# A mixture-of-experts layer: where rows are split for the gather, which buffers are withheld, how many banks the gather turns through, where the loop of further passes stands, and the order of the last step

## The chip, the cores and the metric

The kernel runs on one core of a Trainium2 chip. The metric is the time of one execution on the device, in microseconds (us); the time before is the median of three runs, 1381.6 us (1379.36 to 1382.24).

## The reference

One decoder layer on 256 rows of 2048 numbers, float32 throughout. Causal attention with 16 heads, then `x <- LayerNorm(alpha * x + y)`, then a mixture of 32 experts, then a second such norm. Cut to what matters here, the mixture is:

```python
g_logits = xt @ w_grp + b_grp                  # 4 groups, the best one is taken
e_logits = einsum('td,dge->tge', xt, w_rt)     # 8 experts in it, the best two are taken
comb     = onehot_g[:, :, None] * e_gate[:, None, :]
for g in range(4):
    h = silu(einsum('td,edf->tef', xt, w_gate[g])) * einsum('td,edf->tef', xt, w_up[g])
    y = y + einsum('tef,efd->td', h * comb[:, g, :, None], w_down[g])
```

Each expert has three matrices of 2048 x 512 numbers (4.2 MB each), so the 32 experts are 403 MB that have to be read once; the attention's weights are another 67 MB.

## The kernel before

**Attention.** Weights come through three buffers of 16 KB per partition and are split in two float32r parts on ScalarE and VectorE before TensorE multiplies. None of this part is touched.

**Experts.** Each expert gets room for 64 rows. A step p handles experts 2p and 2p+1, 16 steps in all. In a step, `gather` picks the 64 + 64 rows of the two experts out of the normed rows by products with a one-hot matrix, which puts them transposed into `xg`; VectorE and ScalarE take the sums out of PSUM in turn and apply gain and offset. `gate_up` multiplies `xg` with the gate and up weights, two products at a time beside each other in the array; `hidden` forms silu(gate) * up * weight; `transpose_hidden` turns the result; `second_products` multiplies with the down weights; `add_rows` (called `rest(n)`, one quarter of the columns at a time) scatters the products back to the 256 rows and adds them to `acc`. The `rest` of step p runs between the gate and up products of step p+1, by way of `between`. The gather of step p+1 stands between `gate_up` and `second_products` of step p.

**Rows.** The normed rows are `xn` in float32 (one buffer). Step 0 gathers from `xn`. In step 0 `split_rows_in_three` turns `xn` into three bfloat16 parts (`xb`: two in `hm`, the third in half of the buffer that also holds `xg`), and all later steps gather from the three parts, three products where `xn` took one.

**Buffers.** SBUF is cut in twelve buffers ("slots") of 16 KB per partition. An expert's matrix comes as two loads of 2 MB, each filling one slot. `pieces` lists the loads in order: gate and up of a step, then its down weights; `advance` issues the next ones, on the SyncE queue, whenever `used` hands back slots that TensorE has finished with. Ten slots start the list (`S_FIRST`). Slots 0, 1 and 3 are not handed back once their first load is used (`S_SUM` for `acc`, `S_HM` for `hm`, `S_YS` for `ys_all`), slot 7 holds `xg` and the third part, and slot 4 (`xn`) joins the list in step 0 once the rows are split. So eight slots go round from then on.

**Loop.** An expert with more than 64 rows is served by a loop of further passes (`further_passes`), with a number of rounds read at run time; it stands behind step 10 (`LOOP_AFTER`) and keeps three slots back from loading (`LOOP_SLOTS`, L743 and L768). No weight loads of the loop appear in the trace: it ran no round. The residual alpha * x is added to `acc` in steps 11 and 12, two quarters in each (`RES_AT`, L789 to L792).

**Last step.** The gate and up products of step 15 stand ahead of the second products of step 14, and so do the loads (L418 to L421, L827 to L830). `last_norm` prepares gain and offset of the second norm, ahead of the second products of step 14. The last down weights come in five blocks of columns (`l`), so that the norm can begin early; behind the last products stand the quarters of `rest` of step 14 (L895 to L904).

**Order.** From the last block of the attention's output product on, ScalarE, VectorE and GpSimd run in the order of the code, and from the first gather on TensorE and SyncE too. Each engine is a queue: what stands ahead in the code and waits holds up what follows it on that engine.

Of the kernel before, what the change touches and what calls it, by code (L numbers as in the profile page):

```python
# [29 lines left out]
LOOP_AFTER = 10  # L30
RES_AT = (11, 12)
LOOP_SLOTS = 3
# [6 lines left out]
S_X, S_XT, S_OH, S_OL, S_QK, S_WS, S_TV, S_RING = 0, (1, 2), 3, 4, 5, (6, 7), 8, (9, 10, 11)  # L39


S_XN, S_XG, S_HM, S_SUM, S_YS = S_OL, S_WS[1], S_XT[0], S_X, S_OH
S_FIRST = S_XT + (S_QK,) + S_RING + (S_TV, S_WS[0], S_YS, S_SUM)
# [12 lines left out]
def hybrid_kernel(ctx: ExitStack, tc: tile.TileContext, x, w_qkv, w_o, ln1_g, ln1_b, w_grp, b_grp,  # L56
# [10 lines left out]
    def halves(i, name, dt=F32):  # L67
        t = slot(i, [P, 2, D], name, dt)
        return [t[:, 0], t[:, 1]]
# [82 lines left out]
    ws = Rot([h for i in S_WS for h in halves(i, f"ws{i}", F32R)])  # L152
# [289 lines left out]

    def used(*keys, keep=0):
        free.extend(place[k] for k in keys if place[k] not in (S_HM, S_SUM, S_YS))
        advance(keep)

# [81 lines left out]
    gub, mb, yb = Rot([0, 1]), Rot([2, 3]), (4, 5, 6, 7)  # L528

    def gather(c2, xg, o2, name, xn=None):  # L530
# [19 lines left out]
    def split_rows_in_three():  # L550

        for n in range(2):
            for tt in range(NT):
                t = xn[:, tt, n]
                for i in range(2):
                    nc.scalar.copy(xb[i][:, tt, n], t)
                    nc.vector.tensor_sub(t if i == 0 else xb[2][:, tt, n], t, xb[i][:, tt, n])
# [28 lines left out]
    def gate_up(gu, side, xg, j, wg, wu):  # L586

        for c in range(4 * (j % 2), 4 * (j % 2) + 4):
            st, sp = j == 0 and c == 0, j == 3 and c == 7
            for w, to in ((wg, sides[1 - side]), (wu, sides[side])):  # L590
                nc.tensor.matmul(gu[to], xg(8 * (j // 2) + c), w[:, c, :], start=st, stop=sp, skip_group_check=True)  # L591
# [46 lines left out]
    def residual(n, t):  # L638
# [3 lines left out]
        for tt in range(NT):  # L642
            g_ = rows_of(0, n, yb[2 * tt], f"g1_{n}_{tt}")
# [6 lines left out]
        b_ = rows_of(1, n, yb[0], f"b1_{n}")  # L650
# [24 lines left out]
    def further_passes(slots):  # L675

        ring = Rot(slots[1:])
        n_pass = nc.values_load(passes_i[0:1, 0:1], min_val=0, max_val=8,
                                skip_runtime_bounds_check_because="512 choices in passes of 64 leave at most 7")
        with tc.For_i(0, n_pass, 1, iteration_sync="staggered"):  # L680
# [24 lines left out]
            spare = slot(slots[0], [P, 2, D], "spare")  # L705
            xgx = spare[:, 0, 0:1024].rearrange("p (n e s) -> p n e s", n=NCH, e=1)
# [6 lines left out]
            for j in range(4):  # L713
                if j % 2 == 0:
                    wg, wu = [load([v[one, j // 2].rearrange("o p c f -> p (o c) f")], f"x{i}_{j}", ring())
                              for i, v in enumerate((wg_v, wu_v))]
                gate_up(gu, 0, lambda c: xgx[:, c, 0], j, wg, wu)
# [3 lines left out]
            for k in range(4):  # L721
                if k % 2 == 0:
                    wd = load([wd_v[one, k // 2].rearrange("o p i d -> p (o i) d")], f"xd_{k}", ring())
# [9 lines left out]
    xg_lo = halves(S_XG, "xg_lo")  # L733
    xg = xg_lo[0].rearrange("p (n e s) -> p n e s", n=NCH, e=2)
# [4 lines left out]
    gatef, gate3, xb, o2, scratch, ys_all, acc, rest = (None,) * 8  # L739

    def first_products(p):

        keep = LOOP_SLOTS if p == LOOP_AFTER else 0  # L743
# [233 lines left out]
```

## Time and profile before

| | |
|---|---|
| median of 3 runs | 1381.6 us |
| the profiled execution, its own time | 1382.03 us |
| its span, first to last instruction | 1380.3 us |
| TensorE busy with matmuls | 1307.1 us, 95% of the span |
| VectorE, ScalarE busy | 36%, 25% |
| bytes moved | 475.47 MB, mean 344 GB/s |
| granted TensorE clock, mean | 0.984 |

The profiled execution's own time is 1.7 us more than its span and 0.4 us above the median. TensorE's matmuls are pipelined and their ends are modelled, so 95% busy doesn't say that TensorE is the limit: in the same profile the DMA engines move 425 to 428 GB/s in nearly all slices from the fifteenth on. The page's chain of waits, followed back from the end, names who was last at each point, and the windows say how much was moved in a stretch.

### The profile page before, as it was taken

To read this page: it belongs to the slowest core of one execution; us is meant where nothing else is said; L and a number is where in the kernel's file an instruction comes from. 1 tells how busy PE (TensorE), PEld (TensorE's weight loads), DVE (VectorE), ACT (ScalarE), POOL (GpSimd) and SP (SyncE) were. 2 spreads that over 40 slices of the span, in tenths; PEclk is the share of its full clock that TensorE was granted. 3 is DMA by queue.
4 is the path that set the end of the run, shared out by engine and by line. 5 is a ranking of instruction groups with operands and counts; after the bars stand their busy time and mean duration, and the time that the engine had idled before them with its cause. 6 is when DMAs were issued, how large, how long until landed. Compare 5 with 4: busy or idle time off the path is not lost. (4 is left out here: it accounts for less than half of the span.)

```text
span 1380.3 us, 17486 instructions
## 1 busy us (share of the span) xinstructions
PE 1307.1 (95%) x7433; PEld 738.5 (53%) x7433; DVE 495.8 (36%) x869; ACT 347.6 (25%) x598; POOL 18.1 (1%) x59
## 2 busy tenths in 40 slices
PE   8999999999999999999999999999998799999996
PEld 7888888888896434434434343443433243443432
DVE  5564555545444422122221212222123336222136
ACT  4454534445325301101101010110101010111232
POOL 1000030000000000000000000000000000000000
PEclk9999999999999999999999999999999899999998
DMA  9745545477357999999999999999999999999993
GB/s 320 238 152 185 174 143 185 161 255 270 123 219 278 379 428 426 425 428 425 428 426 426 428 426 426 427 426 427 427 427 425 374 427 426 420 426 424 426 404 118
DMA packets 91829, 475.47 MB, mean 344 GB/s; under 512 B 9252, under 2 KB 48228, under 8 KB 67684
## 3 DMA queue, kind: packets, MB, share of 16 engines
q1 hardware_dynamic: 91748, 474.32, 85.6%
q8 instruction: 60, 0.98, 0.3%
q14 instruction: 21, 0.17, 0.0%
HBM read 472.20 MB, written 2.10 MB: 344 GB/s over the span
## 5 line engine op out<-in xcount | busy, mean ns | idle before, releaser
L591 PE MATMUL gu<-wu,xg_lo 128*64 128x512 f32 x1024 | 465.6, 605 | 15.1 <-DMA wu<-in_moe_w_up_dram 15.1
L591 PE MATMUL gu<-wg,xg_lo 128*64 128x512 f32 x1024 | 465.5, 604 | 8.2 <-PEq L680 8.2
L591 PEld LDWEIGHTS gu<-wg,xg_lo 128*64 128x64 f32 x1024 | 135.6, 138 | 198.7 <-issue 193.5
L764 PE MATMUL y<-wd,ht 128*64 128x512 f32 x960 | 211.4, 594 | 2.7 <-DMA wd<-in_moe_w_down_dram 2.0
L591 PEld LDWEIGHTS gu<-wu,xg_lo 128*64 128x64 f32 x1024 | 135.5, 138 | 100.6 <-issue 68.2
L210 PE MATMUL pj<-xt,ws 128*128 128x512 f32 x512 | 185.0, 403 | 0.0
L163 DVE TENSOR_TENSOR ws<-ring,ws 128x1024 fp32r<-128x1024 f32 x96 | 117.5, 1224 | 128.0 <-ACT ws L162 127.9
L211 PE MATMUL pj<-xt,ws 128*128 128x256 f32 x512 | 147.3, 288 | 0.0
L764 PEld LDWEIGHTS y<-wd,ht 128*64 128x64 f32 x960 | 68.0, 137 | 135.1 <-issue 129.1
L162 ACT CAST ws<-ring 128x1024 fp32r<-128x1024 f32 x96 | 101.1, 1053 | 138.6 <-PE pj L210 59.1
L627 DVE TENSOR_TENSOR acc<-acc,cb 128x512 f32<-128x512 f32 x112 | 71.9, 683 | 171.6 <-PE cb L617 171.6
L210 PEld LDWEIGHTS pj<-xt,ws 128*128 128x128 f32 x512 | 97.7, 191 | 21.8
L610 ACT CAST ys_all<-y 128x512 fp32r<-128x512 f32 x60 | 35.1, 585 | 290.7 <-PE y L764 158.5
L539 PE MATMUL pg<-o_dt.bfloat,hm 128*128 128x128 bf16 x960 | 88.3, 219 | 18.2 <-DVE xg_lo L546 15.5
L611 DVE TENSOR_TENSOR ys_all<-y,ys_all 128x512 fp32r<-128x512 f32 x60 | 41.2, 687 | 174.5 <-ACT ys_all L610 174.5
L211 PEld LDWEIGHTS pj<-xt,ws 128*128 128x128 f32 x512 | 98.5, 192 | 0.3
L539 PEld LDWEIGHTS <-hm 128*128 128x128 bf16 x960 | 75.3, 98 | 37.8 <-issue 37.1
L599 DVE SCALAR_TENSOR_TENSOR hs<-hs,gs,gu 64x512 f32<-64x512 f32 x32 | 23.9, 747 | 191.9 <-ACT hs L598 191.5
L539 PE MATMUL pg<-o_dt.bfloat,xg_lo 128*128 128x128 bf16 x480 | 84.3, 219 | 0.0
L598 ACT ACTIVATE hs<-gu 64x512 f32<-64x512 f32 x32 | 18.9, 591 | 219.5 <-PE gu L591 219.0
L548 ACT ACTIVATE xg_lo<-pg,gbp 128x128 f32<-128x128 f32 x128 | 51.6, 453 | 78.1 <-PE pg L539 78.1
L546 DVE TENSOR_SCALAR xg_lo<-pg,gbp 128x128 f32<-128x128 f32 x128 | 46.6, 406 | 66.2 <-PE pg L539 66.0
(229 smaller groups left out, 1285.3 us busy)
## 6 DMA issues: line engine op xcount, KB each, us to landing
wg<-in_moe_w_gate_dram SPq DMA_DIRECT2D x64, 2048.0 KB, 19.1
wu<-in_moe_w_up_dram SPq DMA_DIRECT2D x64, 2048.0 KB, 23.6
wd<-in_moe_w_down_dram SPq DMA_DIRECT2D x60, 2048.0 KB, 23.3
ring<-in_attn_w_qkv_dram SPq DMA_DIRECT2D x46, 1024.0 KB, 5.3
ring<-in_attn_w_o_dram SPq DMA_DIRECT2D x16, 1024.0 KB, 5.3
wl<-in_moe_w_down_dram SPq DMA_DIRECT2D x6, 1024.0 KB, 15.0
xs<-in_x_dram SPq DMA_DIRECT2D x8, 256.0 KB, 6.8
wl<-in_moe_w_down_dram SPq DMA_DIRECT2D x4, 512.0 KB, 11.5
```

Source lines behind the costliest of these rows:

```text
L162: nc.scalar.copy(t[:, 0, c], src[:, c])
L163: nc.vector.tensor_sub(t[:, 1, c], src[:, c], t[:, 0, c].bitcast(F32))
L210: nc.tensor.matmul(ps[i], w[:, 0], x2, start=c == 0, stop=False, skip_group_check=True)
L211: nc.tensor.matmul(ps[i][:, 0], w[:, 1], x2[:, 0], start=False, stop=c == NCH - 1, skip_group_check=True)
L539: nc.tensor.matmul(pg[:, cc], part[:, tt, n, c], o2[:, tt].rearrange("p e s -> p (e s)"), start=tt == i == 0, stop=tt == 1 and i == len(pa ...
L546: nc.vector.tensor_scalar(to, pg[:, cc], g_, b_, op0=ALU.mult, op1=ALU.add)
L548: nc.scalar.activation(to, pg[:, cc], AF.Identity, scale=g_, bias=b_)
L591: nc.tensor.matmul(gu[to], xg(8 * (j // 2) + c), w[:, c, :], start=st, stop=sp, skip_group_check=True)
L610: nc.scalar.copy(ys[0:rows, 0, 0:width], y[0:rows, 0:width])
L611: nc.vector.tensor_sub(ys[0:rows, 1, 0:width], y[0:rows, 0:width], ys[0:rows, 0, 0:width].bitcast(F32))
L627: nc.vector.tensor_add(t, t, cb)
L764: nc.tensor.matmul(y[n][sides[side]], ht[:, k, sides[side]], held["d", 2 * p + side, k // 2][:, k % 2, n * 512:(n + 1) * 512], start=k == ...
```

## The change

- `xn` stays in its slot until step 4. The gathers for steps 1 to 3 multiply `xn` in float32 (`o2f`, one-hots in float32) as that for step 0 does; the three bfloat16 parts are made in step 3 (`SPLIT_AT`), a quarter at each of the places i = 3 to 6, into the two slots whose weights step 3 has just used (`take`). Gathers from step 4 on use the parts.
- Slot 7 is cut in two halves of its own, one for `xg` and one for `ys_all`. In step 0 only one slot is not handed back, that of down weight (1, 1), for `acc`.
- `gather` turns through four PSUM banks (6, 7, 2, 3; in step 0: 4, 5, 2, 3) rather than two (2, 3). Step 0's last four gathers stand behind i = 1 instead of two each behind i = 0 and i = 1.
- The loop stands behind step 9 and keeps back one slot instead of three; the residual is added in steps 10 to 13, one quarter each, in banks 4, 5 and 6.
- Step 14 and step 15 run in plain order: second products of 14, `last_norm`, gate and up of 15; the loads follow the same order.

```diff
-LOOP_AFTER = 10
-RES_AT = (11, 12)
-LOOP_SLOTS = 3
+SPLIT_AT = 3
+LOOP_AFTER = 9
+RES_AT = (10, 11, 12, 13)
...
-        if pr == NP - 1:
-            pr -= 1
-        elif pr == NP - 2:
-            continue
-        for k in range(2):
-            pieces += [(("d", e, k), [wd_v[e, k]]) for e in (2 * pr, 2 * pr + 1)]
+        if pr < NP - 1:
+            for k in range(2):
+                pieces += [(("d", e, k), [wd_v[e, k]]) for e in (2 * pr, 2 * pr + 1)]
...
     def used(*keys, keep=0):
-        free.extend(place[k] for k in keys if place[k] not in (S_HM, S_SUM, S_YS))
+        free.extend(place[k] for k in keys if k not in taken)
         advance(keep)
...
+    wide, first_banks = Rot([6, 7, 2, 3]), Rot([4, 5, 2, 3])
-        pg = bank(mb(), [P, 2, m], f"pg{name}_{c2}")
-        parts = [xn] if xn is not None else xb
+        pg = bank((banks or mb)(), [P, 2, m], f"pg{name}_{c2}")
+        parts = [xn] if o2.dtype == F32 else xb
...
-        if p == 0 and i < 2:
-            for c2 in (2 * i + 4, 2 * i + 5):
-                gather(c2, xg, o2f, 0, xn)
         if p == 0 and i == 1:
+            for c2 in range(4, 8):
+                gather(c2, xg, o2f, 0, first_banks)
             gatef, gate3 = gates()
...
-            split_rows_in_three()
-        if p == 0 and i == 4:
+        if p == SPLIT_AT and i == 0:
+            take(("g", 2 * p, 0), ("u", 2 * p, 0))
+        if p == SPLIT_AT and i == 1:
+            hm, lo = [slot(place[k, 2 * p, 0], [P, 2, NT, 2, 8, P], f"part_{k}", BF16) for k in "gu"]
+            xb, spare = [hm[:, 0], hm[:, 1], lo[:, 0]], lo[:, 1].rearrange("p t n c a -> p (t n c a)").bitcast(F32)
+        if p == SPLIT_AT and 3 <= i < 7:
+            split_rows_in_three(*divmod(i - 3, 2))
+        if p == SPLIT_AT + 1 and i == 1:
             free.append(S_XN)
             advance()
...
-        if p in RES_AT and i in (4, 6):
-            if i == 4:
-                scratch = sm.tile([P, 64, 8], F32, name=f"xn_{p}", tag="ptv")
-            residual(2 * RES_AT.index(p) + (i - 4) // 2, scratch)
+        if p in RES_AT and i == 5:
+            residual(RES_AT.index(p), sm.tile([P, 64, 8], F32, name=f"xn_{p}", tag="ptv"))
...
-        if p == NP - 2:
-            rest = None
-            hs, last_ot, _ = first_products(p + 1)
-            five, offs = last_norm()
+        if p == 0:
+            place_acc, = take(("d", 1, 1))
         y = second_products(p, ht)
...
-            further_passes(list(free)[:LOOP_SLOTS])
+            further_passes(free[0])
             advance()
-    p, ot = NP - 1, last_ot
+    five, offs = last_norm()
+    hs, ot, *_ = first_products(NP - 1)
+    p, rest = NP - 1, None
...
-    for n in range(2):
-        rest(n)
     for n in range(len(blocks)):
         last_down(n)
...
-            for i in range(2, 4):
-                rest(i)
```

**The order of the loads, first step.** On the SyncE queue, from the first down weight on (the names are wg, wu, wd for gate, up and down, then expert and half; PE, DVE and DMAHW name whom the load waits for), before:

```order
L433 DMA wd_0_0_3261<-in_moe_w_down_dram 128x4096
L433 DMA wd_1_0_3272<-in_moe_w_down_dram 128x4096 [waits DVE_49,Activation_49]
L433 DMA wd_0_1_3395<-in_moe_w_down_dram 128x4096 [waits PE_49]
L433 DMA wd_1_1_3478<-in_moe_w_down_dram 128x4096 [waits DMAHW1_49,PE_49]
L433 DMA wg_2_0_3480<-in_moe_w_gate_dram 128x4096 [waits DMAHW2_49,PE_49]
L433 DMA wu_2_0_3505<-in_moe_w_up_dram 128x4096 [waits DMAHW3_49,DVE_49]
L433 DMA wg_2_1_3515<-in_moe_w_gate_dram 128x4096 [waits DMAHW4_49,PE_49]
```

The same loads in the changed kernel:

```order
L430 DMA wd_0_0_3262<-in_moe_w_down_dram 128x4096
L430 DMA wd_1_0_3273<-in_moe_w_down_dram 128x4096 [waits DVE_49,Activation_49]
L430 DMA wd_0_1_3382<-in_moe_w_down_dram 128x4096 [waits PE_49]
L430 DMA wd_1_1_3384<-in_moe_w_down_dram 128x4096 [waits DMAHW1_49,PE_49]
L430 DMA wg_2_0_3464<-in_moe_w_gate_dram 128x4096 [waits DMAHW2_49,PE_49]
L430 DMA wu_2_0_3466<-in_moe_w_up_dram 128x4096 [waits DMAHW3_49,PE_49]
L430 DMA wg_2_1_3502<-in_moe_w_gate_dram 128x4096 [waits DMAHW4_49,PE_49]
```

The loads keep their order. The up weight wu_2_0 waited for VectorE (the split rows, in the slot of `xn`) and now waits for TensorE; the last number of a name counts the program's instructions, and by it wd_1_1 moves to directly behind wd_0_1, and wu_2_0 to directly behind wg_2_0: each pair is now released at one place.

**The order of the loads, the loop.** On the SyncE queue, the last loads ahead of the loop and the wait in front of it, before:

```order
L433 DMA wd_21_1_6637<-in_moe_w_down_dram 128x4096 [waits DMAHW1_49,PE_49]
L433 DMA wg_22_0_6639<-in_moe_w_gate_dram 128x4096 [waits DMAHW2_49,PE_49]
L433 DMA wu_22_0_6730<-in_moe_w_up_dram 128x4096 [waits DMAHW3_49,PE_49]
L433 DMA wg_22_1_6732<-in_moe_w_gate_dram 128x4096 [waits DMAHW4_49,PE_49]
L433 DMA wu_22_1_6750<-in_moe_w_up_dram 128x4096 [waits DMAHW5_49,PE_49]
L433 DMA wg_23_0_6752<-in_moe_w_gate_dram 128x4096 [waits DMAHW6_49,PE_49]
L678 TENSOR_LOAD passes_i_3324 [waits DVE_49]
L680 COMPARE_AND_BRANCH [waits barrier_Pool_Activation_PE_DVE_SP_release,DMAHW0_49,DMAHW1_49,DMAHW7_49]
```

The same place in the changed kernel:

```order
L430 DMA wd_19_1_6129<-in_moe_w_down_dram 128x4096 [waits DMAHW5_49,PE_49]
L430 DMA wg_20_0_6131<-in_moe_w_gate_dram 128x4096 [waits DMAHW6_49,PE_49]
L430 DMA wu_20_0_6149<-in_moe_w_up_dram 128x4096 [waits DMAHW7_49,PE_49]
L430 DMA wg_20_1_6151<-in_moe_w_gate_dram 128x4096 [waits DMAHW0_49,PE_49]
L430 DMA wu_20_1_6242<-in_moe_w_up_dram 128x4096 [waits DMAHW1_49,PE_49]
L430 DMA wg_21_0_6244<-in_moe_w_gate_dram 128x4096 [waits DMAHW2_49,PE_49]
L430 DMA wu_21_0_6262<-in_moe_w_up_dram 128x4096 [waits DMAHW3_49,PE_49]
L430 DMA wg_21_1_6264<-in_moe_w_gate_dram 128x4096 [waits DMAHW4_49,PE_49]
L682 TENSOR_LOAD passes_i_3325 [waits DVE_49]
L684 COMPARE_AND_BRANCH [waits barrier_Pool_Activation_PE_DVE_SP_release,DMAHW0_49,DMAHW1_49,DMAHW5_49,DMAHW6_49,DMAHW7_49]
```

Five loads stood between the step's last down weight and the loop, seven stand there now. The branch in front of the loop waited for three DMA semaphores, none of which stands beside one of those five loads (they name DMAHW2 to DMAHW6); now it waits for five, and four of them (DMAHW6, 7, 0, 1) stand beside the first four of the seven loads.

**The end, on TensorE.** From the transposed hidden of step 15 to the first block of the last down weights (hp15 is the transposed hidden of step 15, cb14 a scatter of step 14's products, y15_0 the first block), before:

```order
L604 MATMUL hp15_8632<-ident_85,hs15_8474 128x128 x3
L616 MATMUL cb14_0_0_8641<-ys_all_3708,ot14_8272 128x512 [waits DVE_49]
L617 MATMUL cb14_0_0_8641<-ys_all_3708,ot14_8272 128x512
L616 MATMUL cb14_0_1_8645<-ys_all_3708,ot14_8272 128x512 [waits DVE_49]
L617 MATMUL cb14_0_1_8645<-ys_all_3708,ot14_8272 128x512
L616 MATMUL cb14_1_0_8651<-ys_all_3708,ot14_8272 128x512 [waits DVE_49,Activation_49]
L617 MATMUL cb14_1_0_8651<-ys_all_3708,ot14_8272 128x512
L616 MATMUL cb14_1_1_8655<-ys_all_3708,ot14_8272 128x512 [waits DVE_49]
L617 MATMUL cb14_1_1_8655<-ys_all_3708,ot14_8272 128x512
L867 MATMUL y15_0_8661<-wl_0_8545,ht15_8637 64x512 [waits DMAHW5_49,Activation_49]
L867 MATMUL y15_0_8661<-wl_0_8545,ht15_8637 64x512 [waits DMAHW6_49]
L867 MATMUL y15_0_8661<-wl_0_8545,ht15_8637 64x512 x6
```

The same place in the changed kernel:

```order
L595 MATMUL gu15_1_8359<-wg_31_1_8338,xg_3332 64x512
L595 MATMUL gu15_1_8359<-wu_31_1_8387,xg_3332 64x512
L609 MATMUL hp15_8492<-ident_85,hs15_8360 128x128 [waits DVE_49]
L609 MATMUL hp15_8492<-ident_85,hs15_8360 128x128 x3
L870 MATMUL y15_0_8501<-wl_0_8389,ht15_8497 64x512 [waits DMAHW7_49,Activation_49]
L870 MATMUL y15_0_8501<-wl_0_8389,ht15_8497 64x512 [waits DMAHW0_49]
L870 MATMUL y15_0_8501<-wl_0_8389,ht15_8497 64x512 x6
L870 MATMUL y15_1_8517<-wl_1_8426,ht15_8497 64x512 [waits DMAHW1_49]
L870 MATMUL y15_1_8517<-wl_1_8426,ht15_8497 64x512 [waits DMAHW2_49]
L870 MATMUL y15_1_8517<-wl_1_8426,ht15_8497 64x512 x6
```

The eight scatters shown, and eight more of step 14 that stood between the blocks y15_0 and y15_1, are gone from here (they stand between the gate and up products of step 15 now), and the transposed hidden follows directly on the gate and up products that it depends on.

## Rows read from the trace of the kernel before

**Rows 1.** The page: GB/s moved in 40 equal slices of the span.
```profile
GB/s 320 238 152 185 174 143 185 161 255 270 123 219 278 379 428 426 425 428 425 428 426 426 428 426 426 427 426 427 427 427 425 374 427 426 420 426 424 426 404 118
```

**Rows 2.** Windows: length, busy per engine, granted clock, DMA share, GB/s.
```profile
434.00:448.00 14.00, 14.00 (x74) 5.72 (x76) 5.92 (x27) 4.79 (x9) 0.00 (x0) 1.00 0.47 171
...
458.00:463.00 5.00, 4.11 (x38) 2.04 (x35) 3.81 (x9) 4.32 (x7) 0.00 (x0) 1.00 0.43 105
...
700.00:1050.00 350.00, 329.62 (x1818) 140.30 (x1815) 75.13 (x152) 44.25 (x92) 0.00 (x0) 0.99 1.01 427
...
1070.00:1080.00 10.00, 4.78 (x12) 1.64 (x14) 0.52 (x2) 0.00 (x0) 0.71 (x7) 0.54 0.65 239
```

**Rows 3.** Timeline of the SyncE queue, first step: start, length, load, count.
```profile
417.83 29.06 SPq L433 DMA_DIRECT2D wd<-in_moe_w_down_dram  x4
446.99 0.62 SPq L433 DMA_DIRECT2D wg<-in_moe_w_gate_dram  x1
460.08 0.33 SPq L433 DMA_DIRECT2D wu<-in_moe_w_up_dram  x1
```

**Rows 4.** Timeline of TensorE, step 0: two gather pieces from float32 rows.
```profile
431.90 2.05 PE L539 MATMUL pg<-o_dt.float,xn 128*128 128x128 f32 x16
```

**Rows 5.** Chain of waits (start, length, what): one gather from three parts.
```profile
1285.10 0.34 PE r L634 x4
...
1289.14 0.74 DVE xg_lo L546 x2
...
1292.39 1.50 PE pg L539 x24
1293.89 13.88 PE gu L591 x64
```

**Rows 6.** Tile hm: the splitting of the rows (ns min/median/max, first and last start).
```profile
L556 ACT CAST hm<-xn x8: 1028/1043/1045, 441.9 to 457.8; 128x1024 bf16<-128x1024 f32 x8
...
L557 DVE TENSOR_TENSOR xg_lo<-xn,hm x4: 1224/1224/1224, 448.4 to 458.8; 128x1024 bf16<-128x1024 f32 x4
```

**Rows 7.** Timeline of the SyncE queue at the loop.
```profile
1050.41 0.33 SPq L433 DMA_DIRECT2D wg<-in_moe_w_gate_dram  x1
1075.24 0.34 SPq L433 DMA_DIRECT2D wu<-in_moe_w_up_dram  x1
```

**Rows 8.** Waits from 1040 to 1090 us: waiting, waited for, us, times, longest.
```profile
PE gu L591 <- PEq L680: 8.2, 1, 8.2
```

**Rows 9.** Chain of waits: starts of steps 11 to 14 on TensorE.
```profile
1075.22 16.80 PE gu L591 x64
...
1133.60 3.43 PE gu L591 x16
...
1195.51 3.43 PE gu L591 x16
...
1249.98 3.43 PE gu L591 x16
```

**Rows 10.** Chain of waits at the end.
```profile
1308.03 7.04 PE gu L591 x32
1315.07 15.65 DMA wd<-in_moe_w_down_dram
...
1330.76 7.08 PE y L764 x30
1337.84 0.59 PE hp L604 x4
...
1341.01 3.61 PE y L867 x16
...
1347.93 3.58 PE y L867 x16
```

**Rows 11.** Timeline of ScalarE: `last_norm`, its first operation.
```profile
1322.60 2.00 ACT L808 ACTIVATE raw<-wv,rows 5x2048 f32<-5x2048 f32 x1
```

**Rows 12.** Timeline of VectorE: `last_norm`, its last long operation.
```profile
1331.32 2.34 DVE L813 SCALAR_TENSOR_TENSOR five<-raw,rows,five 5x2048 fp32r<-5x2048 f32 x1
```

More of the change, by code (lines that the diff above doesn't have):

```diff
@@ L67, in halves @@
     def halves(i, name, dt=F32):
+        if i == S_LOW:
+            return [slot(f"{i}{k}", [P, D], f"{name}{k}", dt) for k in range(2)]
         t = slot(i, [P, 2, D], name, dt)
@@ L149, in transpose_x @@
         nc.vector.tensor_sub(xt[i][:, k:k + 2, 1], pt, hi.bitcast(F32))
-    ws = Rot([h for i in S_WS for h in halves(i, f"ws{i}", F32R)])
+    ws = Rot([h for i in (S_WS, S_LOW) for h in halves(i, f"ws{i}", F32R)])
     def split_w(wt, half, name, pieces=1, factor=None):
@@ L441, in advance, with take @@
             held[key] = load(srcs, "w" + "_".join(map(str, key)), place[key])
+    taken = set()
     def used(*keys, keep=0):
-        free.extend(place[k] for k in keys if place[k] not in (S_HM, S_SUM, S_YS))
+        free.extend(place[k] for k in keys if k not in taken)
         advance(keep)
+    def take(*keys):
+        taken.update(keys)
+        return [place[k] for k in keys]
     advance(keep=1)
@@ L548, in gather, with split_rows_in_three @@
                 nc.scalar.activation(to, pg[:, cc], AF.Identity, scale=g_, bias=b_)
-    def split_rows_in_three():
-        for n in range(2):
[L553 to L557, printed above, removed]
+    def split_rows_in_three(n, tt):
+        t = xn[:, tt, n]
+        nc.scalar.copy(xb[0][:, tt, n], t)
+        nc.vector.tensor_sub(t, t, xb[0][:, tt, n])
+        nc.scalar.copy(xb[1][:, tt, n], t)
+        nc.vector.tensor_sub(xb[2][:, tt, n], t, xb[1][:, tt, n])
     def in_three(t, part, rest_):
@@ L584, in slots_of, with gate_up @@
         return ot, gs
-    def gate_up(gu, side, xg, j, wg, wu):
-        for c in range(4 * (j % 2), 4 * (j % 2) + 4):
-            st, sp = j == 0 and c == 0, j == 3 and c == 7
+    def gate_up(gu, side, xg, j, wg, wu, at):
+        for c in range(4):
             for w, to in ((wg, sides[1 - side]), (wu, sides[side])):
-                nc.tensor.matmul(gu[to], xg(8 * (j // 2) + c), w[:, c, :], start=st, stop=sp, skip_group_check=True)
+                nc.tensor.matmul(gu[to], xg(4 * j + c), w[:, at + c, :], start=j == c == 0, stop=j == c == 3,
+                                 skip_group_check=True)
     def hidden(gu, side, gs, hs):
@@ L673, in gates, with further_passes @@
         return gate, gate3
-    def further_passes(slots):
-        ring = Rot(slots[1:])
+    def further_passes(last):
         n_pass = nc.values_load(passes_i[0:1, 0:1], min_val=0, max_val=8,
@@ L713, in further_passes @@
             for j in range(4):
[L714 to L717, printed above, removed]
+                c = slice(4 * (j % 2), 4 * (j % 2) + 4)
+                w = load([v[one, j // 2][:, :, c].rearrange("o p c f -> p (o c) f") for v in (wg_v, wu_v)], f"x{j}", last)
+                gate_up(gu, 0, lambda c: xgx[:, c, 0], j, w[:, 0], w[:, 1], 0)
             hidden(gu, 0, gs, hs)
@@ L722, in further_passes @@
                 if k % 2 == 0:
-                    wd = load([wd_v[one, k // 2].rearrange("o p i d -> p (o i) d")], f"xd_{k}", ring())
+                    wd = load([wd_v[one, k // 2].rearrange("o p i d -> p (o i) d")], f"xd_{k}", last)
                 for n in range(4):
@@ L797, in last_norm @@
     def last_norm():
-        raw, high = halves(S_HM, "raw")
-        five = halves(S_XG, "five", F32R)[0]
+        raw, high = halves(place["g", 2 * SPLIT_AT, 0], "raw")
+        five = halves(place["u", 2 * SPLIT_AT, 0], "five", F32R)[0]
         r5, h5, f5 = raw[0:5, :], high[0:5, :].bitcast(F32R), five[0:5, :]
@@ L825, in hybrid_kernel @@
             for c2 in range(split_at, 8):
-                gather(c2, xg, o2, p + 1)
-        if p == NP - 2:
-            rest = None
-            hs, last_ot, _ = first_products(p + 1)
-            five, offs = last_norm()
+                gather(c2, xg, og, p + 1, wide)
+        if p == 0:
+            place_acc, = take(("d", 1, 1))
         y = second_products(p, ht)
         if p == 0:
-            ys_all = slot(S_YS, [P, 2, 2, 512], "ys_all", F32R)
-            acc = halves(S_SUM, "acc")
+            ys_all = slot(f"{S_LOW}1", [P, 2, 2, 512], "ys_all", F32R)
+            acc = halves(place_acc, "acc")
         def rest(n, p=p, y=y, ot=ot):
@@ L893, in weigh @@
             nc.vector.tensor_mul(acc[tt][:, cs], acc[tt][:, cs], g2[:, cs])
-    for n in range(2):
-        rest(n)
     for n in range(len(blocks)):
```

40 lines of the change are left out of this document (18 added, 22 removed).

## The prediction

> **What bounds the kernel now.** I read the page first. Its slices say that from the fifteenth on (483 us) the DMA engines move 425 to 428 GB/s almost without a break, and that the slices ahead of that, where the experts begin, reach 123, 219, 278 and 379 [rows 1]. The long window from 700 to 1050 us gives the full rate, 427 GB/s [rows 2]. A load of 2 MB (2.097 million bytes) therefore costs 4.9 us, a step's twelve cost 58.9 us, and every microsecond in which nothing flows after the first experts' loads is added to the end, unless TensorE is later still. So I looked next for pauses. The windows show three places: between 434 and 448 us 171 GB/s flow, which is 14 x (1 - 171/427) = 8.4 us of full rate lost; between 458 and 463 us 105 GB/s, 3.8 us; between 1070 and 1080 us, at the loop, 239 GB/s, 4.4 us [rows 2].
>
> What ends the first two is read from the SyncE queue: four down loads take from 417.8 to 446.9 us to be issued, and the up load at 460.08 us stands for 12.5 us behind the gate load that ended at 447.6 [rows 3]. These loads had no slot. The first of them waited for a pair of weights of which only one slot came back, the last for slot 4, which the splitting of the rows held until its last subtraction had begun at 458.8 us [rows 6].
>
> Then TensorE. From step start to step start it needs 61.9 us in step 12 (two quarters of the residual) and 54.5 us in step 13 (none) [rows 9], against the 58.9 us of the loads. So it is slower than the loads only around the loop and the residual, and it catches up by the end: there the chain goes through the last down load of step 14, issued at 1315.07 us, landed at 1330.7 [rows 10]. DMA and TensorE are close to a draw at the end, which is the main risk of what follows.
>
> **The change part by part.** All against the span of the profiled execution, 1380.3 us.
>
> *Step 0: slots.* In place of one load the first release brings two, and that at 447 us brings two more at once; the next, one pair of gate and up products later (7.04 us [rows 10], so at about 454), no longer stands behind slot 4. In the 14 us from 434 to 448, two loads flow instead of one and a little: 14 - 2 x 4.9 = 4.2 us lost instead of 8.4. The 3.8 us from 458 on are covered, since after 447 us two loads (9.8 us) last until past that release. With nine slots going round, the loads then run dry again just before the first down halves of step 0 are used up (I put 0.7 us). Gain 8.4 + 3.8 - 4.2 - 0.7 = 7.3 us. Bounds: 12.2 us if no pause is left, and 0 if all of it is taken back as below.
>
> *Steps 1 to 3: gathers from float32.* A gather piece from `xn` takes 2.05 / 2 = 1.02 us [rows 4], the eight of a step 8.2 us; one pair of pieces from three parts takes 1.50 us [rows 5], eight 6.0 us. But today's gather takes from 1285.44 to 1293.89 us, 8.45 us, because two banks make it wait for VectorE to empty them (0.74 us twice for a piece pair [rows 5]). With four banks the float32 gather is bound by its products: 8.2 + 0.6 us for the transposes [rows 10], 8.8 us, 0.4 us more than now in each of three steps. From step 4 on four banks give 6.0 + 0.6 = 6.6 us, 1.8 us less for TensorE in each step.
>
> *Steps 3 and 4: two slots taken, the split.* From the taking in step 3 until `xn` is freed in step 4, seven slots go round. Counted load by load at 4.9 us from 447 us on, some three and a half loads have landed when TensorE starts step 3, at about 593 us; so the queue runs dry for about 1 us when the taken pair brings no release. The split is 16 operations of 1.04 and 1.22 us [rows 6] in a chain that took 441.9 to 460.0 us, four quarters of about 3.7 us; in step 3 the last three come behind each other after i = 3 and end some 3 us after TensorE wants the second half of the gather, which costs another 1 us of release. I take 2.5 us lost in steps 1 to 4, with 0 and 7.3 as ends (nothing, or all that step 0 gained).
>
> *The loop.* Before it, the last load is issued at 1050.41 us and the next at 1075.24 [rows 7]; TensorE stands for 8.2 us [rows 8]. Keeping back one slot rather than three puts two more loads, 9.8 us, into the pause of 4.4 us: it goes. What is late next: the branch in front of the loop now waits for the first four of the seven loads ahead of it, the last of which lands 4 x 4.9 = 19.6 us after the step's last down weight; today the loop is left about 23 us after that landing (7.08 us for the last half of the second products [rows 10]; four gather pieces of 0.75 us, sixteen scatters and the waits between, estimated at 8 us; 8.2 us of standing), so this wait ends inside it. Three loads are then still to come, 14.7 us. Gain 4.4 us, ends 0 and 4.4. The loop's standing on TensorE stays, and with it the clock: 0.54 granted in that window, so 1.2 GHz for nearly all of it [rows 2], and 16.80 us for 64 products [rows 9] that take 13.88 at 2.4 GHz [rows 5].
>
> *Residual.* Step 11 and 12 lose two quarters each, steps 10 to 13 get one each: (61.9 - 54.5) / 2 = 3.7 us at today's price. More banks can only lower that, so TensorE's steps behind the loop come to 54.5 + 3.7 - 1.8 = 56.4 us, under the loads' 58.9. From leaving the loop (23 us after the last down landing of step 9) TensorE reaches the end of step 14's second products after 23 + 58.4 - 3.7 - 1.8 (step 10, with the slow clock that step 11 has now in its 58.4 us from 1075.22 to 1133.60 [rows 9]) + 3 x 56.4 + 55.5 (step 14: as step 13, 1.8 us less for the gather and 2.8 us more for the copies of gain and offset) = 300.6 us; the loads allow it at 5 x 58.9 + 7 = 301.6. So DMA sets it, by a hair.
>
> *The end.* The load that counts is now the last up weight of step 15, as many bytes from the start as the last down weight of step 14 was (order and bytes of all that follows are the same). Behind it: 7.04 us of gate and up products instead of 7.08 of second products, then silu, product, transposes and copy, 2.8 us, against the 3.1 us from 1337.84 to 1341.01 today. Then the scatters of step 14 are gone from between the first two blocks: 1347.93 - 1344.62 = 3.3 us [rows 10]. `last_norm` takes ScalarE and VectorE from 1322.60 to 1333.66, 11 us [rows 11, 12], and now stands ahead of step 15's scatters on both; TensorE stalls there for some 3 us, with the wait for the loads of step 15 beside it. Gain 3.3 + 0.3, of which I keep 3.0; ends -3 (if the stall shows whole) and 3.6.
>
> Sum: 7.3 - 2.5 + 4.4 + 3.0 = 12.2 us; span 1368.1, and with the 1.7 us around it a time of 1369.8 us, against 1382.0 for that execution and a median of 1381.6.
>
> The new second one-hot matrices, the halves of slot 7, the smaller loop body and the move of `acc` cost nothing: VectorE is busy 36% and idle where the one-hots are made, the loop runs no round, and the others move no instruction.
>
> **The rivals.** *TensorE becomes the end* (chance 0.15). The draw of 300.6 against 301.6 us could tip: four banks may save less, since ScalarE and VectorE are held by `hidden` when the gather begins. Without the 1.8 us in five steps TensorE is 9 us later; less the 1.0 us in hand and about 2 us that the stall in step 15 absorbs, the time is about 1376.
>
> *The slots are taken back* (0.12). For: seven slots for a whole step, one less than now. Against: the rate stayed at 427 GB/s with eight, and TensorE then still has loads in hand. If the whole 7.3 us is lost in steps 3 and 4, the time is 1369.8 + 4.8 = 1374.6.
>
> *The clock falls in the waits of step 15* (0.05). The profile has the low level only after the 8.2 us at the loop; in 700 to 1050 us, where TensorE also waits for loads, 0.99 is granted [rows 2]. If it falls once, the loop's price is the measure: 16.80 - 13.88 = 2.9 us, time 1372.7. The Trainium skill (TensorE: Matmul & The Clock Gate, HAM oscillation) says that bursts of products with waits for DMA between them can each start cold; by that rule the last pair of step 15 would be at the low level and take 14 us. The long window of this trace speaks against it.
>
> *The loop gets longer: slower* (0.08). The branch waits for loads in flight, which it didn't before. If it takes all seven instead of four, SyncE leaves after 34.3 us rather than 23, TensorE stands 11 us longer, nothing is in flight for the first load's way, and the 1.0 us in hand is gone: 1369.8 + 11.3 - 1.0 + the 4.4 us of pause again = 1384.5. It decides from a leaving time of about 31 us after the last down landing on. Against it: the semaphores named are those of four loads.
>
> **How the numbers follow.** Forecast 0.60, rivals 0.15, 0.12, 0.05, 0.08. The range goes from 1364 (step 0's 12.2 us, less 1 lost, 4.4, 3.6 gained: about 1363) up to 1379, past the first three rivals and short of the last. Faster by over 0.2% (2.8 us, about what can be told from no change) holds for the forecast and nearly all of the first three: 0.84; within it 0.08, slower 0.08.
>
> **What would show it.** Of the changed kernel: 434 to 448 us at about 300 GB/s and no dip at 458; no dip under 400 GB/s at the loop, with TensorE still standing 8 us; a short dip in step 3 at about 611 us; gather pieces of 1.0 us in steps 1 to 3 and gathers of under 7 us later; the first block of the last down weights starting at about 1332 us and the second right behind it. Wrong would be: DMA under 420 GB/s for long after step 3, TensorE without waits from the loop to the end, or a loop left more than 31 us after the down weight landed.

## The result, and the profile after

The changed kernel takes 1368.3 us (median of four executions, 1366.7 to 1370.0) against 1381.9 before (four executions too): a ratio of 0.990, 95% interval 0.9875 to 0.9926. The forecast was 1369.8 us, in a range of 1364 to 1379. The profiled execution took 1366.67 us with a span of 1365.0 us, 15.3 us shorter than that of before.

Its 40 slices of the span, GB/s, answer to [rows 1]: the tenth slice is unchanged (270), the thirteenth and fourteenth carry 361 and 412 where 278 and 379 stood, and the dip of 374 at the loop is gone.

```profile
GB/s 320 245 154 185 166 158 182 157 253 270 141 196 361 412 419 426 427 426 425 426 428 425 427 427 426 426 426 427 427 425 424 427 427 426 428 425 427 427 391 115
```

The windows of [rows 2] again, with that of the seven-slot stage (605 to 620), the loop (now at 1000 to 1010) and the end (1325 to 1335); columns as there.

```profile
434.00:448.00 14.00, 14.00 (x76) 5.62 (x75) 6.66 (x33) 5.32 (x10) 0.00 (x0) 1.00 0.99 395
458.00:463.00 5.00, 5.00 (x47) 5.00 (x46) 2.39 (x7) 2.21 (x6) 0.00 (x0) 1.00 1.02 434
605.00:620.00 15.00, 15.00 (x74) 5.32 (x72) 10.93 (x14) 7.21 (x9) 0.00 (x0) 1.00 1.00 421
700.00:950.00 250.00, 235.46 (x1303) 103.60 (x1300) 54.94 (x111) 31.00 (x65) 0.00 (x0) 0.99 1.01 426
1000.00:1010.00 10.00, 8.29 (x26) 2.97 (x28) 0.52 (x2) 0.00 (x0) 0.71 (x7) 0.66 1.01 421
1325.00:1335.00 10.00, 8.48 (x34) 2.95 (x36) 1.45 (x2) 2.66 (x4) 0.00 (x0) 0.83 0.96 334
```

The SyncE queue in step 0 and at the loop answers to [rows 3, 7]: the four down loads go out within 17.2 us rather than 29.1, and the last load ahead of the loop at 987.1 with seven in flight.

```profile
415.42 17.24 SPq L430 DMA_DIRECT2D wd<-in_moe_w_down_dram  x4
442.64 0.33 SPq L430 DMA_DIRECT2D wg<-in_moe_w_gate_dram  x1
...
987.13 0.33 SPq L430 DMA_DIRECT2D wg<-in_moe_w_gate_dram  x1
1006.50 0.34 SPq L430 DMA_DIRECT2D wu<-in_moe_w_up_dram  x1
```

At the loop TensorE still stands, 6.2 us after 8.2 [rows 8].

```profile
PE gu L595 <- PEq L684: 6.2, 1, 6.2
```

To see where the 15.3 us come from I cut each execution at the landing of the same loads: load 8 (the last gate load issued ahead of the first down load), load 20 (the last up load of step 1), load 36, and load 187, the last but one of the full-sized expert loads. Landings are read from the DMA records one by one; 12 loads at the full rate take 58.9 us.

```
us                         to load 8  8 to 20  20 to 36  36 to 187  187 to end   span
before                        425.5     72.8      78.5      749.0       54.5    1380.3
changed                       423.3     63.5      78.9      746.7       52.7    1365.0
changed, a second time        423.5     63.5      80.7      746.6       51.0    1365.3
two_banks                     421.7     63.4      81.6      748.2       51.1    1365.9
two_banks_late                425.1     62.7      79.9      747.0       52.8    1367.5
loop_three                    424.5     62.7      80.2      747.4       52.7    1367.5
old_last                      424.3     63.5      80.5      747.1       56.4    1371.8
split_step0                   425.9     76.4      78.5      746.6       52.8    1380.2
split_step1                   424.3     62.8      88.2      746.8       52.8    1374.8
one_slot_later                425.6     67.5      78.9      746.7       51.0    1369.6
```

The first stretch holds only work that no variant touches, so its 421.7 to 425.9 us are chance: 2.2 us of the 15.3 are that. The rest is 9.3 us in step 0, 0.4 lost in the next sixteen loads, 2.3 from load 36 on (2.1 of them around the loop, where 24 landings took 121.4 us and now take 119.3), and 1.8 at the end. The second profile of the changed kernel has 2.2 lost in place of the 0.4 and 3.5 gained at the end in place of the 1.8, so single stretches repeat to within about 2 us only. The same first gain in a window from landing 8 to landing 20, of before and of the changed kernel: 25.6 and 25.7 MB, in 72.8 us and in 63.5.

```profile
425.50:498.30 72.80, 70.45 (x414) 30.98 (x416) 27.18 (x62) 22.38 (x37) 0.00 (x0) 1.00 0.85 351
```

```profile
423.30:486.80 63.50, 63.40 (x348) 29.33 (x346) 15.06 (x51) 13.74 (x28) 0.00 (x0) 1.00 0.98 405
```

### The profile page after: what moved, and what is told of

The parts are those of the page before. It is cut to its first block, busy times and chain, and to the rows that moved or that the text cites. A ratio compares the mean times of both kernels' runs of the same rounds, so it can differ in the third digit from the quotient of the medians.

```text
span 1365.0 us, 17314 instructions
## 1 busy us (share of the span) xinstructions
PE 1305.1 (96%) x7337; PEld 749.1 (55%) x7337; DVE 497.3 (36%) x875; ACT 347.1 (25%) x598; POOL 18.7 (1%) x59
## 5 line engine op out<-in xcount | busy, mean ns | idle before, releaser
L595 PE MATMUL gu<-wu,xg 128*64 128x512 f32 x1024 | 462.5, 601 | 24.2 <-DMA wu<-in_moe_w_up_dram 24.2
L595 PE MATMUL gu<-wg,xg 128*64 128x512 f32 x1024 | 464.3, 601 | 6.2 <-PEq L684 6.2
L595 PEld LDWEIGHTS gu<-wg,xg 128*64 128x64 f32 x1024 | 134.3, 138 | 183.3 <-issue 173.6
L595 PEld LDWEIGHTS gu<-wu,xg 128*64 128x64 f32 x1024 | 134.4, 138 | 122.3 <-issue 72.9
L766 PEld LDWEIGHTS y<-wd,ht 128*64 128x64 f32 x960 | 71.3, 137 | 128.4 <-issue 121.1
L544 PE MATMUL pg<-o_dt.bfloat,part_g 128*128 128x128 bf16 x768 | 68.6, 219 | 3.1 <-ACT ht L611 2.9
L544 PEld LDWEIGHTS <-part_g 128*128 128x128 bf16 x768 | 59.3, 98 | 15.2 <-issue 15.1
L553 ACT ACTIVATE xg<-pg,gbp 128x128 f32<-128x128 f32 x128 | 51.7, 454 | 58.5 <-PE pg L544 58.3
L544 PE MATMUL pg<-o_dt.bfloat,part_u 128*128 128x128 bf16 x384 | 66.3, 219 | 0.0
L551 DVE TENSOR_SCALAR xg<-pg,gbp 128x128 f32<-128x128 f32 x128 | 46.4, 406 | 40.9 <-PE pg L544 40.7
## 6 DMA issues: line engine op xcount, KB each, us to landing
wu<-in_moe_w_up_dram SPq DMA_DIRECT2D x64, 2048.0 KB, 25.6
```

The source lines that it names most:

```text
L544: nc.tensor.matmul(pg[:, cc], part[:, tt, n, c], o2[:, tt].rearrange("p e s -> p (e s)"), start=tt == i == 0, stop=tt == 1 and i == len(pa ...
L551: nc.vector.tensor_scalar(to, pg[:, cc], g_, b_, op0=ALU.mult, op1=ALU.add)
L553: nc.scalar.activation(to, pg[:, cc], AF.Identity, scale=g_, bias=b_)
L595: nc.tensor.matmul(gu[to], xg(4 * j + c), w[:, at + c, :], start=j == c == 0, stop=j == c == 3, skip_group_check=True)
L766: nc.tensor.matmul(y[n][sides[side]], ht[:, k, sides[side]], held["d", 2 * p + side, k // 2][:, k % 2, n * 512:(n + 1) * 512], start=k == ...
```

## The experiments

All are edits of the changed kernel, timed in three series, each with the kernel before in it: its median was 1382.4 us beside split_step0, two_banks, loop_three and old_last, 1381.3 beside one_slot_later, half_last, warm_last and half_warm, and 1380.9 beside the rest. The changed kernel (1368.3 us) was timed in its first measurement and again in the last series, not in the first two. There a difference of about 2 us from it is an indication only, and the stretches between landings have to decide.

**The split back in step 0.**

```diff
-SPLIT_AT = 3
+SPLIT_AT = 0
...
+        if p == SPLIT_AT and i == 1:
+            for q in range(4):
+                split_rows_in_three(*divmod(q, 2))
         if p == SPLIT_AT and 3 <= i < 7:
-            split_rows_in_three(*divmod(i - 3, 2))
-        if p == SPLIT_AT + 1 and i == 1:
+            pass
+        if p == SPLIT_AT and i == 4:
```

> The changed kernel with the rows split in bfloat16 in the first step as before (the pair of slots taken there, the float32 rows given up half a step later; from then on the gathers are those of three parts). Theory A (all that the slots gave in the first step stays to the end): the loads from the eighth to the twentieth take 9 us longer to land, as they did before, and the time is 1377.4. Rival B (the prediction's sum for the slots, 7.3 less 2.5 given back): 1373.1. Rival C (the loads catch up later, since the queue is deep again from step 2 on): 1368.3 to 1370.

Measured: 1379.3 us (ratio to before 0.9972, 0.9962 to 0.9982), 11.0 us slower than the changed kernel. Between the landings the whole difference stands from 8 to 20 (76.4 us), and none of it is made up later (746.6 us from load 36 on, as in the changed kernel). It is 3.6 us worse there than before, because this edit keeps both slots of the first released pair, where before one came back: the third down load goes out at 445.5 us here, at 437.6 before. The four down loads again take 28 us to go out:

```profile
418.26 28.03 SPq L430 DMA_DIRECT2D wd<-in_moe_w_down_dram  x4
```

**One slot back later.**

```diff
-        free.extend(place[k] for k in keys if k not in taken)
+        free.extend(place[k] for k in keys if k not in taken and k != ("u", 0, 0))
...
+        if p == 0 and i == 4:
+            free.append(place["u", 0, 0])
+            advance()
```

> The changed kernel, but of the first pair of weights used up only one slot comes back at once, as before; the other comes back after five of the step's eight quarter products (some 18 us later), all else as changed. Theory A (what the loads lose in the first step stays to the end): the load that went out at 432.3 us waits for the next release at 442.6 and one load time is lost, 4.9 us; time 1373.2. Rival B (the queue refills later, so the loss is made up): 1368.3 to 1369.

Measured: 1369.8 us (0.991, 0.9896 to 0.9925), 1.5 us slower. The loads lose 4.0 us up to load 20, not 4.9, and keep that loss to load 187; the end is 1.7 us shorter than in the changed kernel's profile (the clock did not fall there, below). So theory A holds between the landings, and the median shows less of it than the trace does; the two intervals overlap. Part of that may be the next stretch: from load 8 to load 36 it is 146.4 us here, 142.4 and 144.2 in the two profiles of the changed kernel, so 2.2 to 4.0 us are lost.

```profile
418.06 27.55 SPq L430 DMA_DIRECT2D wd<-in_moe_w_down_dram  x4
```

**The split in step 1**, `SPLIT_AT = 1` in place of 3.

> The changed kernel with the pair of slots taken and the rows split in step 1 rather than step 3. Theory A (the queue is still shallow there: the load at 487 us could go out only with the next release at 496, when the last one in flight has landed at 492): some 3 to 5 us lost between the twentieth and the thirty-sixth landing, 1372. Rival B (the prediction's term for this stage wherever it stands): 2.5 us, 1370.8. Rival C (seven slots are enough): 1368.3.

Measured: 1375.8 us (0.996, 0.9946 to 0.9975), 7.5 us slower, more than any theory said. Seven slots are not enough there: behind the taken pair the four down loads take 26.2 us to go out and the rate falls to 227 GB/s for 20 us, 20 x (1 - 227/427) = 9.4 us.

```profile
479.99 26.19 SPq L430 DMA_DIRECT2D wd<-in_moe_w_down_dram  x4
```

```profile
480.00:500.00 20.00, 20.00 (x90) 7.45 (x88) 9.12 (x15) 4.29 (x7) 0.00 (x0) 1.00 0.56 227
```

Two steps later the same stage lost 0.2 us by the rate (421 GB/s from 605 to 620).

**Two banks.** In all gathers behind the first, and then only from step 4 on:

```diff
-    wide, first_banks = Rot([6, 7, 2, 3]), Rot([4, 5, 2, 3])
+    wide, first_banks = mb, Rot([4, 5, 2, 3])
```

```diff
-            gather(c2, xg, og, p + 1, wide)
+            gather(c2, xg, og, p + 1, wide if p < SPLIT_AT else mb)
```

> The changed kernel, with the gathers of the steps behind the first going through two PSUM banks again instead of four. Theory A (the loads set the time from 445 to 1315 us and TensorE has time in hand): each such gather takes about 2 us longer (8.4 instead of 6.3 us from step 4 on, a little over 9 in steps 1 to 3), TensorE's waits for loads in steps 12 to 15 get shorter by as much, and the time stays within 1 us of the changed kernel's 1368.3. Rival B (the draw between TensorE and the loads, as the prediction priced it): TensorE is late by 1.8 us in each of five steps behind the loop, less some 3 us that it has in hand, so 1374 to 1376.

> Four banks for the gathers of steps 1 to 3 only, two again from step 4 on. Theory A (the banks pay in steps 1 to 4, where TensorE never waits and so paces the slots: with two banks the loads from the twentieth to the hundred-and-eighty-seventh took 829.8 us instead of 825.5): no loss to speak of, 825.5 us between those landings and 1368.3. Rival B (the prediction: the gain of the banks is 1.8 us for each gather from step 4 on): 829 us, or TensorE without waits in steps 12 to 15, and 1370.5 or more.

Measured: 1370.5 us (0.9916, 0.9902 to 0.993) and 1368.5 us (0.9907, 0.9892 to 0.9922). Neither theory on the first was right: two banks cost about 2 us, but not because TensorE ends late. What they cost stands between landings 20 and 64: 222.0 us, against 217.7 and 219.4 in the two profiles of the changed kernel and 218.3 in two_banks_late. In the window of step 3 (605 to 620) two_banks has 395 GB/s, where the changed kernel has 421 and 422. In that of step 1 (480 to 500) its 395 stand against 414 and 401, which is too close to tell:

```profile
480.00:500.00 20.00, 20.00 (x92) 7.55 (x90) 7.84 (x17) 2.14 (x4) 0.00 (x0) 1.00 0.97 395
605.00:620.00 15.00, 15.00 (x74) 5.32 (x72) 11.47 (x16) 7.03 (x9) 0.00 (x0) 1.00 0.96 395
```

There TensorE is busy without a break and hands the slots back, so by this reading its gathers pace the loads. From the first piece to the second products, the float32 gather of step 1 takes 8.15 us with four banks and 9.43 with two (timeline of TensorE, changed kernel first):

```profile
456.68 5.62 PE L544 MATMUL pg<-o_dt.float,xn 128*128 128x128 f32 x48
...
464.83 3.65 PE L766 MATMUL y<-wd,ht 128*64 128x512 f32 x16
```

```profile
455.49 2.05 PE L544 MATMUL pg<-o_dt.float,xn 128*128 128x128 f32 x16
457.81 4.17 PE L544 MATMUL pg<-o_dt.float,xn 128*128 128x128 f32 x32 [0.27 <-DVE xg L551]
...
462.94 2.05 PE L544 MATMUL pg<-o_dt.float,xn 128*128 128x128 f32 x16 [0.51 <-ACT xg L553]
464.92 3.65 PE L766 MATMUL y<-wd,ht 128*64 128x512 f32 x16
```

From step 4 on the banks are worth nothing in time (1368.5 against 1368.3 us in the same series), only TensorE's waits change. These are TensorE's longest between 1100 and 1316 us (us in total, times, longest), of before, of the changed kernel and of two_banks_late:

```profile
PE pg L539 <- DVE xg_lo L546: 5.0, 8, 1.3
PE b L634 <- DVE acc L649: 4.5, 3, 1.9
```

```profile
PE gu L595 <- DMA wu<-in_moe_w_up_dram: 7.4, 7, 1.9
```

```profile
PE pg L544 <- DVE xg L551: 3.3, 6, 1.3
...
PE gu L595 <- DMA wu<-in_moe_w_up_dram: 2.3, 3, 1.0
```

Before, TensorE waited for no load in this stretch; now it waits 7.4 us for them, and 2.3 with two banks. The loads set the time in both.

**Three slots kept at the loop.**

```diff
+LOOP_SLOTS = 3
...
-        keep = p == LOOP_AFTER
+        keep = LOOP_SLOTS if p == LOOP_AFTER else 0
...
```

> The changed kernel, with three slots kept back at the loop as before instead of one. Theory A (what counts is the time between landings of successive loads, which before was 41.3 us for the eight across the loop where 39.2 is the usual): 2.1 us slower than the changed kernel, about 1370.4, and a visible dip of the rate in the window at the loop all the same. Rival B (the rate in the window counts, 239 GB/s over 10 us, as the prediction priced it): 4.4 us slower, 1372.7. Rival C: nothing, because TensorE stands at the loop anyway: 1368.3.

Measured: 1370.5 us (0.9919, 0.9905 to 0.9932), 2.1 us slower, theory A's number, though the intervals overlap and the changed kernel was not in this series. No load goes out for 23 us and the rate falls to 301 GB/s over 10 us (3.0 us of full rate), while the 24 landings across the loop take only 0.4 us longer (119.7 against 119.3). So what the two slots alone give stays open between 0.4 and 2.1 us; the loop also moved from step 10 to step 9 and the residual was spread, and no run takes these back.

```profile
982.01 0.33 SPq L431 DMA_DIRECT2D wg<-in_moe_w_gate_dram  x1
1005.02 0.34 SPq L431 DMA_DIRECT2D wu<-in_moe_w_up_dram  x1
```

```profile
1000.00:1010.00 10.00, 5.12 (x16) 1.92 (x18) 0.52 (x2) 0.00 (x0) 0.71 (x7) 0.66 0.79 301
```

**The old order at the end** (loads, products and the scatters between the first blocks as before).

```diff
...
+        if p == NP - 2:
+            rest = None
+            hs, last_ot, *_ = first_products(p + 1)
+            five, offs = last_norm()
...
-    five, offs = last_norm()
-    hs, ot, *_ = first_products(NP - 1)
...
```

> The changed kernel with the order of the end as before: the gate and up products of the last step ahead of the second products of the one before it, its rows scattered between the first blocks of the last down weights. Theory A (the traces: the end came 15.3 us earlier, of which the last full load accounts for 13.5): 1.8 us slower than the changed kernel, 1370.1. Rival B (the prediction's term): 3.0 us slower, 1371.3. Rival C (the wait for silu, transposes and a slow clock eats the gain of the plain order): same, 1368.3.

Measured: 1372.1 us (0.9925, 0.9912 to 0.9939), 3.7 us slower, nearest to theory B. The chain of its end and that of the changed kernel (start, length, what):

```profile
1297.16 23.12 DMA wd<-in_moe_w_down_dram
1320.33 8.78 PE y L770 x30
...
1332.27 3.61 PE y L876 x16
...
1339.19 3.58 PE y L876 x16
...
1343.90 3.61 PE y L876 x16
```

```profile
1296.21 21.03 DMA wu<-in_moe_w_up_dram
...
1317.29 7.09 PE gu L595 x30
...
1325.84 0.67 PE hp L609 x4
...
1327.17 8.78 PE y L870 x32
...
1337.09 3.61 PE y L870 x16
```

From the landing of the last full load (1320.3 and 1317.2) to the third block it is 23.6 us in the old order and 19.8 in the new. In both 8.78 us stand where 32 such products can take 7.09: both are slowed alike, with 0.81 of the clock granted.

**The clock at the end, and smaller last loads.** Idle products in TensorE's waits of step 15:

```diff
+    keep_warm(20, 6, zero)
     ht = transpose_hidden(hs, p)
+    keep_warm(8, 7, zero)
```

> The changed kernel with idle products (20 of 128 by 128 by 128, some 0.07 us each) put on TensorE in the last step where it waits for silu and the product (1.47 us), and 8 where it waits for the copy of the transposes (0.67 us). Theory A (the waits take the clock down, and the first two down blocks then take 8.78 us rather than 7.09, as in one of the variants where the wait ahead of them was missing): 1.7 us less, 1366.6. Rival B (the wait for the load before it is enough to take the clock down, or the blocks wait for their weights anyway): 1368.3.

Measured: 1368.6 us (0.9908, 0.9892 to 0.9925): no change in the median. In the profile the first two blocks take 7.09 us and the granted clock stays at 1.00:

```profile
1329.40 7.09 PE y L872 x32
```

```profile
1325.00:1335.00 10.00, 9.53 (x64) 4.23 (x62) 1.45 (x2) 3.04 (x5) 0.00 (x0) 1.00 1.02 350
```

The unedited kernel a second time says why so little of it shows:

> The changed kernel once more, unedited, beside the variants that follow: 1368.3 us as before if what lies between executions is chance (the eighth load landed between 421.7 and 426.6 us in the variants, whose work up to there is the same); the profile then tells whether the 8.78 us of the first two down blocks come back each time or not.

Measured: 1368.3 us (0.9908, 0.9894 to 0.9922). This time its blocks took 7.09 us as well, behind the same waits. So the clock falls there in some executions only, and the 1.7 us are lost in those. Of the nine profiles with this order at the end and no idle products, six show 0.80 or 0.81 granted in these blocks and three 1.00; the three with idle products all show 1.00. That the idle products hold the clock is likely by this count, and not shown.

```profile
1329.19 7.09 PE y L870 x32
```

The last pair of gate and up weights as two mixed halves, and both edits together:

```diff
+                if e == NE - 1 and j:
+                    for h in range(2):
+                        c = slice(4 * h, 4 * h + 4)
+                        pieces += [(("h", h), [wg_v[e, j][:, c], wu_v[e, j][:, c]])]
...
```

> The changed kernel, with the last pair of gate and up weights (4 MB in two loads of 2 MB, all of gate ahead of all of up) loaded as two pieces of 2 MB that each hold half of gate and half of up. Theory A (the end is the last full load plus the products that need it): 3.65 us of products instead of 7.08 behind the landing at 1317.3, so 3.4 us less, 1364.9. Theory B (the clock falls in the new wait between the two pieces): half of that is lost again, 1366.5. Rival C (the last down blocks, which land from 1322.6 to 1339.2 us, become the bound): no gain, 1368.3.

> Both of these together. If each works for itself: 3.4 and 1.7 us less, 1363.2. If the last down blocks' landing at 1339.2 us takes over as the bound (1.95 us of products, then the same 18 us as now behind the last block's start at 1344.7 us): not under 1362.8. If only one of them works, 1364.9 or 1366.6.

Measured: 1367.6 us (0.9894, 0.9877 to 0.9911) and 1365.1 us (0.9882, 0.9866 to 0.9899). Alone the halves gave 0.7 us in the medians, which is within the spread, not 3.4. Cut at the last full landing they gave 2.5: from there to the third block it is 17.3 us, against 19.8 in the changed kernel at the same slow clock. The chain of half_last has no load behind 1263 us: it goes through `last_norm` to the first scatter of step 15, after which TensorE multiplies 13.9 us on end and finishes 4.7 us behind the last landing (1322.5), where the products that need it take 3.65; and its blocks took 8.68 us. In this variant TensorE had become the end, the prediction's first rival, by way of the stall behind `last_norm`. The intervals of the two runs overlap, so it is not shown that the idle products add to the halves.

```profile
1299.32 2.34 DVE five L826
...
1313.28 13.91 PE gu L600 x64
...
1329.97 8.68 PE y L880 x32
```

**A faster version.** The halves for the first four experts and the last, with the idle products:

```diff
+FINE = (0, 1, 2, 3, NE - 1)
...
+                if e in FINE:
+                    for h in range(2):
+                        c = slice(4 * h, 4 * h + 4)
+                        pieces += [(("h", e, 2 * j + h), [wg_v[e, j][:, c], wu_v[e, j][:, c]])]
...
```

> As half_warm, with the pieces of half gate and half up used for all of the first four experts and the last one, so that the first two steps give back one slot every 3.65 us of products instead of two every 7.1. Theory A (the loads of the first step wait for slots alone): the eighth to the twentieth landing 61 us instead of 62.7 to 63.5, time 1363.5 against half_warm's 1365.1. Rival B (the same number of slots per step, so nothing): 1365.1. Rival C (twice the DMAs of half the size cost SyncE or the queues more than they give): 1366 or more.

Measured: 1364.2 us (0.9877, 0.986 to 0.9894), 4.1 us under the changed kernel beside it. From load 8 to the same point as load 20 it is 61.9 us against 62.7 in half_warm; the 0.9 us between their medians are within the spread, so theories A and B are not told apart. The third block now waits for its weights (4.29 us rather than 3.61; its second load lands at 1334.8).

```profile
1309.27 13.91 PE gu L601 x64
...
1325.97 7.17 PE y L883 x32
...
1334.27 4.29 PE y L883 x16
```

## Why the prediction was right, point by point

**The frame held.** The expert loads set the time, a pause early on is not made up behind load 36 (746.6 to 748.2 us from load 36 to load 187 in every variant of the table, 749.0 before), and the sum of 12.2 us stands against 13.6 in the medians. The terms were off on both sides, so that the sum came this close is in part luck.

**Step 0: 7.3 us forecast, 9.3 between the landings.** The window from 434 to 448 carried 395 GB/s, not 300. The count of "two loads" there left out the rest of the load issued at 424 and the first part of the pair of 442.6. The dip at 458 went, as said.

**Steps 1 to 4: 2.5 us lost forecast, 0.4 and 2.2 in the two profiles.** This term failed: the queue was to run dry in steps 3 and 4, and from load 36 to load 64, which covers them, it is 138.8 us before and 138.8 and 138.6 in the two profiles. The little that is lost stands earlier, from load 20 to load 36. The float32 gather was not 0.4 us longer than now but 0.3 shorter (8.15 against 8.45), since with four banks its copies run beside the products. With two banks a loss comes (140.4 us from load 36 to load 64), and with the split in step 1 a larger one: 7.5 us, about the bound of 7.3.

**The loop: 4.4 us forecast, about 2 found** (2.1 between the landings of before and after). The step that failed is to price a pause by the window's rate: 4.4 us by the rate were 2.1 between the landings, and in loop_three 3.0 were 0.4. How much of the 2.1 the two slots gave stays open. The wait of the branch went as worked out: SyncE left 25.9 us behind the last down landing (980.6 to 1006.5), where 23 was said and 31 would have decided for the fourth rival.

**The end: 3.0 us forecast, 3.7 by old_last,** of which the profile shows 1.8, for there the clock took 1.7 back. At equal clock the stretch behind load 187 gives nearly the same twice, 3.5 and 3.7: 54.5 us before against 51.0 in changed_again, both at full clock, and 56.4 in old_last against 52.7, both slowed. The working's upper end of 3.6 was right and the stall behind `last_norm` was hidden in the wait for loads, as assumed.

**The rivals.** TensorE is not the end: it waits for loads in steps 12 to 15, and even with two banks from step 4 on. The draw was less close than said: 1.0 us in hand was forecast, and TensorE waits 7.4 us for loads there, 2.3 with two banks. half_last, which brings the last load's work forward, tips it. The slots were not taken back: from load 20 to load 187 it is 825.5 and 827.3 us, 827.5 before. The rival of the clock, given 0.05, came true in part, inside the forecast: granted 0.83 from 1325 to 1335 us (a mean of time at 2.4 and at 1.2 GHz) and 8.78 us for 7.09, a price of 1.7 and not 2.9. The forecast left that out. The argument against it, 0.99 in the long window, looked at waits for loads, and the wait for the load (here 1.2 us) is not what it takes: in half_last TensorE multiplied for 13.9 us on end, waited 1.5 us for silu and 0.7 for the copy, and the blocks behind that took 8.68 us at 0.81. The Trainium skill (TensorE: Matmul & The Clock Gate, HAM oscillation) says that waits for DMA between bursts of products can leave the next burst cold; here the burst right behind that wait ran at full speed (7.09 us from 1317.29), and the slow one stood behind the waits for VectorE and ScalarE. changed_again, with the same waits, shows that it need not happen (7.09 us). What decides between the two was not found.

## What to carry to other kernels

A kernel that streams weights through a fixed set of buffers has two regimes: while the queue is shallow, whatever frees a buffer sets the time (here who holds a slot and, by two_banks, TensorE's gathers), and behind that the bytes do. Work that takes buffers away belongs where the queue is deep: the same stage cost nothing to speak of in step 3, 7.5 us in step 1 and 11 in step 0. Price a pause from landing to landing of the same loads rather than by a window's rate, and cut the span at such landings before comparing two executions, so that chance ahead of the change is not credited to it.

## What was not expected of the hardware

A load issued into an empty queue takes 8.1 to 8.4 us to land (460.08 to 468.18 and 1075.24 to 1083.62 before), one in a full queue 4.9 us after the one before it. TensorE's clock fell, in some executions only, behind waits of 1.5 and 0.7 us, in half_last without a wait for a load just ahead of them. Identical work ahead of load 8 ended between 421.7 and 426.6 us.
